# A self-planned hybrid decoder layer: state space kept in place, H by rows of both groups, and a planner with new costs

## The chip, the cores and the metric

The kernel runs on one core of a Trainium2 chip. Its metric is device time in microseconds, from the first to the last instruction as the host's timing of the device sees it; the time before is the median of 3 runs. TensorE (PE) multiplies matrices into PSUM, VectorE (DVE), ScalarE (ACT) and GpSimd (POOL) do the element-wise work, SyncE (SP) issues nearly all DMAs, in one queue and in order.

## The reference

One decoder layer on x of 2048 rows by 1024 (float32), one batch. After an RMSNorm one projection gives q, k, v (512 columns each) and u (512):

```python
proj = hn @ w_in[l]
q, k, v, u = jnp.split(proj, [QK_WIDTH, 2 * QK_WIDTH, 2 * QK_WIDTH + V_WIDTH], axis=-1)
q = partial_rope(...); k = partial_rope(...)          # first 16 of 64 columns rotated
attn = diff_attention(q, k, v, lam)                   # 4 heads, two softmax maps each, p0 - lam * p1, causal
attn = rms_norm(attn, subln_g[l]) * (1.0 - lambda_init)
ssm = s5_mixer(u, ...)
mixed = jnp.concatenate([attn, ssm], axis=-1) @ w_out[l]
h = h + mixed
hn = rms_norm(h, norm2_g[l])
h = h + (jax.nn.silu(hn @ w_gate[l]) * (hn @ w_up[l])) @ w_down[l]
return rms_norm(h, final_g)
```

The state space mixer has 32 groups of 16 channels; each drives a 64-wide complex diagonal state by a scan over positions. Then y = Re(C state) + D u, GELU, and a gate: `y * sigmoid(y @ w_glu + b_glu)`.

## The kernel before

All products in float32 are split into a high and a low part (`split`: ACT copies the high part, DVE subtracts) and made of three matmuls (`mm3`, lines 488 to 490).

**The planner.** The Python program does not write instructions in their final order. `Sched` holds tasks with an engine (or a choice of engines), a cost in microseconds, a priority and rings of buffers that they take and give; `run` simulates the engines with these costs, with `LAT0` and `MORE0` as latencies between engines and a formula for DMAs, and issues each task's instructions as its simulated turn comes. Each engine then executes its own list strictly in that order and waits on semaphores. `Rec` records the code of the first phase (projection and state space) as such tasks, with costs by a formula in `call`; all its instructions carry line 349 in the profile, so there one goes by tiles: `pair`, `pv`, `fx`, `tp` are PSUM banks, `hn` and `misc` SBUF areas that are carved again in each stage.

**Projection and state space** (`phase1`). Priorities run: norm, u's columns, tables of the state space (`ssm_prep`, two halves of 16 groups), 16 pairs of groups (`ssm_pair`), then the columns of q and k without rotation, those of v in two halves of 256, and last the rotated columns of q and k. As TensorE needs little time for the state space, the projection's matmuls stand between its pieces. A pair n loads u, G, H, T and E; TensorE makes z = G u (into `pv`) and y = T u (into `fx`); ACT copies z's halves so that real and imaginary parts stand together; DVE multiplies with cosine and sine tables that POOL builds, scans, multiplies back and writes the state into a PSUM bank (`tp`) in four instructions on 64 partitions that also swap the halves of odd and even groups; the state is split, TensorE adds H times the state to y, GELU goes to `yD` in DRAM. T is loaded into a scratch tile and copied by POOL in another order. Positions are blocked: index s (0 to 7) inside a step, c (0 to 255) over steps, position 8c + s.

**Gate** (`glu`). In 8 blocks b of 256 positions: four loads of y (line 1433) gather, for 128 channels each, 8 pieces of 32 numbers per channel; matmuls with w_glu; Tanh and a product (line 1474) write through a permuted view into the order of positions; `mixD`. The output projection's second half (`outproj(1, ...)`, with x added, result in `hD`) follows; these have low priority and fill gaps of attention.

**Attention** (`scores`, `values`). By head and block of 256 queries, for 128 queries at a time: scores into a PSUM pair, row maxima on DVE (line 1167), Exp on ACT (line 1182). Over 1024 keys a row has two pieces; ACT makes the factor between their maxima (line 1185), DVE adds the sums (lines 1201, 1203), forms the factor of the second map (1208, 1209) and, for the first piece, another (1212). Mixes of 512 columns (lines 1227 to 1235) join both maps on DVE or POOL, whichever the planner expects to be ready sooner. Transposes (line 1264), a split and products with v follow. q is loaded by four DMAs into one of two tiles (line 1102), k by line 1107, v by line 1112.

**After attention.** `outproj(0, ...)` reads `hD`, adds attention's half, and `norm2` norms and transposes; the FFN works by Strassen's scheme on halves (lines 1613 on) and the planner orders it in the same way.

Of the kernel before, what the change touches and what calls it, by code (L numbers as in the profile page):

```python
# [20 lines left out]
S = 2048  # L21
# [13 lines left out]
MORE0 = dict(pe=dict(dve=0.07, act=0.13, pool=0.12), pool=dict(dve=0.07))  # L35
# [136 lines left out]
class Sched:  # L172
# [13 lines left out]
    def __call__(self, engs, cost, fn, *deps, take=(), give=(), pri=0.0, size=0, stream=0, of=(), bias=BIAS):  # L186
# [62 lines left out]
    def run(self, until=None):  # L249
        while until is None or not until.done:  # L250
# [31 lines left out]
class Rec:  # L282


    def __init__(self, S, nc):
        self.S, self.real, self.pri, self.mem, self.open = S, nc, 0.0, {}, []
        self.areas, self.turned = {}, {}
# [78 lines left out]
    def call(self, eng, f, args, kw):  # L366
# [27 lines left out]
        if f == "tensor_tensor_scan":  # L394
            cost["dve"] *= 1.0
        if kw.get("op") == ALU.pow:
            cost["pool"] += 0.25 + 0.09 * n
        if eng == "any":
            return self.task({e: cost[e] for e in ("dve", "pool")}, [c])
# [70 lines left out]
class K:  # L470
# [72 lines left out]
    def setup(self, ctx):  # L543
# [10 lines left out]
        self.mixD = d("mixD", [128, 16, 8, 128])  # L554
        self.GHD = [d(f"GHD{i}", [128, 16, 2, 2, 128]) for i in range(2)]
# [39 lines left out]
    def phase1(self):  # L595
# [115 lines left out]
        rec.pri = -50.0  # L711
# [6 lines left out]
        rec.pri = -40.0  # L718
# [38 lines left out]
        for b in range(NB):  # L757
# [3 lines left out]
            for key in (("q", 0), ("k", 0)):  # L761
                t = proj(key, b, mm[2:4])
# [10 lines left out]
            self.hn_end.append(S.join(*rec.users(*(a.tile for a in self.hnb[b]))))  # L773
# [61 lines left out]
    def ssm_prep(self, pp, hf):  # L835
# [9 lines left out]
        if True:  # L845
# [87 lines left out]
            for q0 in range(0, NG, 2):  # L933
# [23 lines left out]
                nc.sync.dma_start(out=self.GHD[hf][:, gs], in_=gh.bitcast(F32))  # L957
# [4 lines left out]
            wh = view(self.gh2[0][:, 0:512], [128, 2] + B3[1:], F32R)  # L962
            self.split(wh[:, 0], wh[:, 1], wt)
            nc.sync.dma_start(out=self.WD[hf][112:240], in_=wh.bitcast(F32).rearrange("p j g h -> p j (g h)"))
# [5 lines left out]
    def ssm_pair(self, n):  # L970
# [11 lines left out]
        for i, z in enumerate((G, H)):  # L982
            nc.sync.dma_start(out=z.bitcast(F32), in_=self.GHD[hf][:, 2 * n8:2 * n8 + 2, i])
        if n % 2 == 0:

            self.T = s1.tile([128, 2, 4, 8, 16], F32R, name="sT")
            wd = self.WD[hf]
            for j in range(2):
                tr = s2.tile([128, 8, 4, 16], F32, name="tr")
                src = bass.AP(tensor=wd.tensor, offset=256 * j + 32 * n8, ap=[[512, 128], [16 * 512, 8], [1, 64]])  # L990
# [39 lines left out]
        v.tensor_tensor(out=t2, in0=pq, in1=Sb, op=ALU.mult)  # L1030
# [3 lines left out]
        for i in range(2):  # L1034
            v.tensor_tensor_scan(out=pq[:, i], data0=r, data1=t1[:, i], initial=0.0, op0=ALU.mult, op1=ALU.add)
        t1 = s2.tile(P3, F32, name="t1")
        t2 = s2.tile(P3, F32, name="t2")
        v.tensor_tensor(out=t1, in0=pq, in1=Cb, op=ALU.mult)
        v.tensor_tensor(out=t2, in0=pq, in1=Sb, op=ALU.mult)
# [7 lines left out]
        self.split(xh[:, :, 1:], xl[:, :, 1:], xs[:, :, 0:255])  # L1047
# [3 lines left out]
        a_.activation(out=gy, in_=y, func=AF.Gelu_apprx_tanh)  # L1051
# [4 lines left out]
    def phase2(self, upto=9):  # L1056
# [60 lines left out]
        def scores(pri, q, kk, j, t, l1c, over):  # L1117
# [12 lines left out]
            for ms in ((0, 1),) if L <= 512 else ((0,), (1,)):  # L1130
                for ci, c0 in enumerate(range(0, lt, 1024)):
# [27 lines left out]
                    def top(y, x=x, ms=ms, ci=ci, w=w):  # L1159
# [8 lines left out]
                        if ci:  # L1168
                            v.tensor_tensor(out=nl[:, i:i + 1], in0=nl[:, i - 1:i], in1=nl[:, i:i + 1], op=ALU.min)

                    y = S("dve", len(ms) * w * 1.042e-3 + 0.06 + (0.2 if ci else 0.0), top, x,
                          take=[] if first else [stats], pri=pri)
                    if not first:
                        first.append(y)
                    rings = [(U if ci else P)[m] for m in ms]

                    def exp(z, x=x, ms=ms, ci=ci, w=w, rings=rings):
# [6 lines left out]
                        if ci:  # L1184
# [894 lines left out]
```

## Time and profile before

| what | value |
|---|---|
| median of 3 runs | 2558.77 us (2556.92 to 2560.48) |
| the profiled execution | 2562.99 us, span 2561.2 us, granted clock 0.97 |
| q1, nearly all DMAs | 304464 packets, 384.39 MB, 48.0% of 16 engines |
| HBM | 259.08 MB read, 129.70 MB written |

The profile is of one execution. Busy time is the union of an engine's instructions; a group's row gives count, busy us and mean ns, then idle time just before the group and what ended it. Rows of the timeline give start and duration in us, engine, line, operation, output<-inputs, and in brackets the wait before. Rows of one line's instructions give minimum/median/maximum ns and the first and last start. A wait is put down to the semaphore that came last. The granted clock is the share of TensorE's full clock that it was given.

### The profile page before, as it was taken

The numbers are of one execution on the slowest core, as the hardware profiler recorded it, in microseconds if no ns is written. First come the engines' busy times: TensorE is split into PE (matmuls) and PEld (weight loads), VectorE is DVE, ScalarE is ACT, GpSimd is POOL, SyncE is SP. The second block draws the span as 40 slices with busy tenths as digits, with TensorE's granted clock in tenths as the row PEclk, the third lists the DMA queues.
The fourth block names the chain that finished last, engine by engine and source line by source line (L and its number), as shares of the span: only waits on it lengthen the run. The fifth ranks groups of instructions, "written<-read, shape, count | busy, mean of one in ns | idle before, by whom it ended". The sixth has DMA issues, their size and how long they took to land.

```text
span 2561.2 us, 34139 instructions
## 1 busy us (share of the span) xinstructions
PE 2355.5 (92%) x11736; PEld 1955.0 (76%) x11736; DVE 1805.1 (70%) x2898; ACT 997.5 (39%) x1971; POOL 1015.3 (40%) x1013
## 2 busy tenths in 40 slices
PE   7998789878998998997999999899999989989997
PEld 6787678757887777876788888788888867868775
DVE  7886884157999987558655655775655686695886
ACT  6222332246666555345333333343333332332343
POOL 4323561345665555336422222432222234253252
PEclk9999899989999999999999999999999989999999
DMA  5556675555547558588422222332222235555553
GB/s 196 163 173 213 193 211 156 152 179 156 138 140 222 169 174 233 180 290 275 127 83 73 93 82 82 116 116 83 83 87 79 85 125 172 178 181 165 187 173 126
DMA packets 307230, 391.03 MB, mean 153 GB/s; under 512 B 71984, under 2 KB 209264, under 8 KB 307056
## 3 DMA queue, kind: packets, MB, share of 16 engines
q1 hardware_dynamic: 304464, 384.39, 48.0%
q10 hardware_dynamic: 2592, 4.45, 0.5%
q8 instruction: 93, 1.52, 0.2%
q14 instruction: 81, 0.66, 0.1%
HBM read 259.08 MB, written 129.70 MB: 152 GB/s over the span
## 4 chain that ended last, share of the span: by engine, by line
PE 59%; DVE 19%; DMA 10%; issue 4%; POOL 3%; ACT 2%; SPq 1%; POOLq 0%; ACTq 0%; DVEq 0%
PE pair L488 8%; PE pair L489 8%; PE pair L490 8%; PE pair L349 6%; PE tp L490 3%; PE tp L489 3%; PE tp L488 3%; DVE misc L349 3%; DMA misc<-uD 3%; PE fx L488 2%; PE pv L490 2%; PE pv L489 2%; PE pv L488 2%; PE fx L490 2%; PE fx L489 2%
## 5 line engine op out<-in xcount | busy, mean ns | idle before, releaser
L1708 ACT CAST misc<-hn 128x512 fp32r<-128x512 f32 (+1 forms) x340 | 202.9, 609 | 479.4 <-POOL hn L1772 198.7
L488 PE MATMUL pair<-hn,misc 128*128 128x512 f32 x925 | 365.0, 395 | 17.2 <-DVE misc L1997 8.6
L490 PE MATMUL pair<-hn,misc 128*128 128x512 f32 x925 | 364.7, 394 | 8.3 <-DVE misc L1709 8.3
L489 PE MATMUL pair<-hn,misc 128*128 128x512 f32 x925 | 364.7, 394 | 7.6 <-DVE hn L1709 7.6
L1709 DVE TENSOR_TENSOR misc<-hn,misc 128x512 fp32r<-128x512 f32 (+1 forms) x340 | 250.6, 744 | 136.0 <-ACT misc L1708 135.7
L349 PE MATMUL pair<-hn,misc 128*128 128x512 f32 x1152 | 283.9, 402 | 2.6 <-DVE misc L349 2.6
L349 PEld LDWEIGHTS pair<-hn,misc 128*128 128x128 f32 x1152 | 219.0, 193 | 51.1 <-DVE misc L349 3.7
L488 PEld LDWEIGHTS pair<-hn,misc 128*128 128x128 f32 x925 | 176.0, 190 | 57.7 <-ACT misc L2006 8.5
L1182 ACT ACTIVATE hn<-pair,small 128x1024 f32<-128x1024 f32 (+4 forms) x192 | 166.3, 868 | 134.8 <-DVE small L1167 72.4
L489 PEld LDWEIGHTS pair<-hn,misc 128*128 128x128 f32 x925 | 176.0, 190 | 47.6 <-DVE hn L1709 11.3
L490 PEld LDWEIGHTS pair<-hn,misc 128*128 128x128 f32 x925 | 175.9, 190 | 47.7 <-DVE misc L1709 11.4
L1772 POOL TENSOR_TENSOR hn<-misc,hn 128x512 f32<-128x512 f32 (+1 forms) x68 | 90.8, 1335 | 283.4 <-DVE misc L1709 277.3
L1769 POOL TENSOR_TENSOR misc<-hn 128x512 f32<-128x512 f32 (+1 forms) x68 | 87.8, 1291 | 256.5 <-DVE misc L1709 191.9
L489 PE MATMUL tp<-hn,misc 128*128 128x512 f32 x457 | 179.8, 393 | 5.8 <-DVE hn L1709 5.8
L1779 POOL TENSOR_TENSOR hn<-hn 128x512 f32<-128x512 f32 (+1 forms) x68 | 95.7, 1407 | 221.3 <-DVE misc L1709 221.3
L488 PE MATMUL tp<-hn,misc 128*128 128x512 f32 x457 | 179.7, 393 | 1.2 <-ACT misc L2006 1.2
L490 PE MATMUL tp<-hn,misc 128*128 128x512 f32 x457 | 179.4, 393 | 0.9 <-DVE misc L1709 0.9
L1820 DVE TENSOR_TENSOR misc<-pair,misc 128x512 f32<-128x512 f32 x156 | 106.9, 688 | 99.7 <-PE pair L490 99.7
L1167 DVE TENSOR_REDUCE small<-pair 128x1 f32<-128x1024 f32 (+7 forms) x160 | 157.6, 988 | 21.8 <-PE pair L1149 11.5
L1229 POOL TENSOR_SCALAR hn<-hn,small 128x512 f32<-128x512 f32 (+3 forms) x105 | 80.8, 769 | 193.7 <-DVE small L1209 137.9
L349 POOL TENSOR_TENSOR misc<-misc 128x256 f32<-128x256 f32 (+1 forms) x128 | 116.8, 921 | 51.3 <-DVE misc L349 27.6
L349 DVE TENSOR_TENSOR misc<-misc,misc 128x512 f32<-128x512 f32 (+5 forms) x122 | 88.9, 754 | 52.0 <-ACT misc L349 47.4
(268 smaller groups left out, 5777.4 us busy)
## 6 DMA issues: line engine op xcount, KB each, us to landing
hn<-vD SPq DMA_DIRECT2D x48, 512.0 KB
hn<-kD SPq DMA_DIRECT2D x96, 256.0 KB
hn<-in_w_gate SPq DMA_DIRECT2D x44, 512.0 KB
hn<-in_w_up SPq DMA_DIRECT2D x44, 512.0 KB
fD<-misc SPq DMA_DIRECT2D x88, 256.0 KB
hn<-qD SPq DMA_DIRECT2D x128, 128.0 KB
hD<-misc SPq DMA_DIRECT2D x32, 512.0 KB
misc<-hD SPq DMA_DIRECT2D x32, 512.0 KB
```

Of the source, the lines that this page charges most:

```text
L349: getattr(ENGINE[t.at](self.real), f)(*map(now, args), **{n: now(x) for n, x in kw.items()})
L488: nc.tensor.matmul(out, lhsT=ah, rhs=bh, start=start, stop=False, **k)
L489: nc.tensor.matmul(out, lhsT=ah, rhs=bl, start=False, stop=False, **k)
L490: nc.tensor.matmul(out, lhsT=al, rhs=bh, start=False, stop=stop, **k)
L1167: v.tensor_reduce(out=nl[:, i:i + 1], in_=x.got[sc][:, 0:w], axis=AX.X, op=ALU.max, negate=True)
L1182: a_.activation(out=z.got[rings[i]][:, 0:w], in_=x.got[sc][:, 512 * i:512 * i + w], func=AF.Exp, bias=st(n, n + 1), accum_out=acc)
L1708: hf = lambda t: a_.copy(out=dst(t)[0], in_=src())
L1709: lf = lambda t: (g_ if t.at == "pool" else v).tensor_sub(out=dst(t)[1], in0=src(), in1=dst(t)[0].bitcast(F32))
L1769: s1 = any_(n, lambda t, e: e.tensor_tensor(out=t.got[s1r][:, 0:n], in0=q(1, 0), in1=q(1, 1), op=ALU.add), *r, take=[s1r], pri=pri())
L1772: s2 = any_(n, lambda t, e: e.tensor_sub(out=q(0, 0), in0=s1.got[s1r][:, 0:n], in1=q(0, 0)), s1, s3, a11, pri=pri())
L1779: s4 = any_(n, lambda t, e: e.tensor_sub(out=q(0, 1), in0=q(0, 1), in1=q(0, 0)), s2, a12, pri=pri())
L1820: return S("dve", 1.042e-3 * w + 0.07, lambda t: v.tensor_tensor(out=(t if to is None else to).got[tm], in0=x.got[bank], in1=y.got[tm], op ...
```

## The change

1. **Planner.** Latencies to TensorE are raised by 0.1 us, each task of the other engines costs 0.09 to 0.13 more, DMAs are counted slower, and the costs of recorded instructions get a formula by kind and by use of PSUM. Choices between DVE and POOL in the state space use the factor `FAIR` (1.2 on DVE) in place of `BIAS` (4).
2. **State space.** The scan and the multiplication back stay in SBUF tiles of all 128 partitions: no state in PSUM and no swap. H is stored as rows of both groups (`HD`), and H's product runs on 64 rows at a time, two halves per group. y of the two groups stands in two banks (`fx`, and the `tp` bank that the state had). T is stored so that its load needs no copy; its weights are read with a step of four. The multiplications by sine may run on DVE or POOL. `ssm_prep` stores G once and H twice where it stored both at once.
3. **Projection's end.** The second half of v's columns goes behind the rotated columns of q and k.
4. **Gate.** A block b is now the index s of the position, so that y comes in one load of pieces of 256 numbers, nothing is permuted, and the result goes to `sD`. The output projection's tile i takes rows z, s (every eighth position); its first part waits for the eight stores of its half.
5. **Attention.** ACT adds the sums, POOL forms the factor of the second map, the separate factor (1212) is gone, and the scaling of the first map's first piece becomes a task of its own on ACT or POOL.

```diff
-MORE0 = dict(pe=dict(dve=0.07, act=0.13, pool=0.12), pool=dict(dve=0.07))
+MORE0 = dict(pe=dict(dve=0.17, act=0.23, pool=0.22), pool=dict(dve=0.07))
+STEP = dict(dve=0.09, act=0.09, pool=0.13)
...
-                self.dma = max(self.dma, s + 1.1) + t.size / 3.6e5
-                t.end = self.dma + 0.95
+                self.dma = max(self.dma, s + 1.5) + t.size / 2.8e5
+                t.end = self.dma + 1.5
...
-        cost = dict(dve=1.042e-3 * n + 0.07, act=0.88e-3 * n + (0.16 if "accum_out" in kw else 0.08),
-                    pool=(1.1e-3 if f == "tensor_scalar" else 0.3e-3 if f == "memset" else 2.2e-3) * n + 0.1)
+        if f == "tensor_tensor_scan" or psum[0]:
+            dve = 2.3e-3 * n + 0.03
+        elif f in ("tensor_scalar", "memset"):
+            dve = 0.75e-3 * n + 0.03
+        else:
+            dve = 1.06e-3 * n + 0.06 if any(psum) else 1.27e-3 * n + 0.02
+        cost = dict(dve=dve, act=0.87e-3 * n + (0.26 if "accum_out" in kw else 0.08),
+                    pool=(1.0e-3 if f == "tensor_scalar" else 0.3e-3 if f == "memset" else 2.0e-3) * n + 0.12)
... # ssm_prep
-                nc.sync.dma_start(out=self.GHD[hf][:, gs], in_=gh.bitcast(F32))
+                nc.sync.dma_start(out=self.GD[hf][:, gs], in_=gh[:, :, 0])
+                for f in range(2):
+                    nc.sync.dma_start(out=self.HD[hf][gs, :, f].rearrange("g p x -> p g x"),
+                                      in_=gh[64 * f:64 * f + 64, :, 1])
... # ssm_pair
-                tr = s2.tile([128, 8, 4, 16], F32, name="tr")
-                nc.sync.dma_start(out=tr.rearrange("p s g h -> p s (g h)"), in_=src)
-                g_.tensor_scalar(out=self.T[:, j].rearrange("p g s h -> p s g h"), in0=tr, scalar1=1.0, scalar2=1.0,
-                                 op0=ALU.mult, op1=ALU.mult)
+                nc.sync.dma_start(out=self.T[:, j].bitcast(F32).rearrange("p (s x) -> p s x", s=8), in_=src)
...
-        y = view(self.fx1, P3, F32)
+        y = [z[:, 0:256] for z in (self.fx1, self.tp2[1])]
-            self.mm3(y[:, g], T[:, 0, tg], T[:, 1, tg], u[:, g, :, 0], u[:, g, :, 1], g == 0, True, skip_group_check=True)
+            self.mm3(y[g], T[:, 0, tg::4], T[:, 1, tg::4], u[:, g, :, 0], u[:, g, :, 1], True, True)
...
-        v.tensor_tensor(out=t2, in0=pq, in1=Sb, op=ALU.mult)
-        xs = view(self.tp2[1], P3, F32)
-        v.tensor_tensor(out=xs[lo, 0], in0=t1[lo, 0], in1=t2[lo, 1], op=ALU.subtract)
-        v.tensor_tensor(out=xs[hi, 1], in0=t1[hi, 0], in1=t2[hi, 1], op=ALU.subtract)
-        v.tensor_tensor(out=xs[hi, 0], in0=t1[lo, 1], in1=t2[lo, 0], op=ALU.add)
-        v.tensor_tensor(out=xs[lo, 1], in0=t1[hi, 1], in1=t2[hi, 0], op=ALU.add)
+        nc.any.tensor_tensor(out=t2, in0=pq, in1=Sb, op=ALU.mult)
+        v.tensor_tensor(out=t1[:, 0], in0=t1[:, 0], in1=t2[:, 1], op=ALU.subtract)
+        v.tensor_tensor(out=t1[:, 1], in0=t1[:, 1], in1=t2[:, 0], op=ALU.add)
...
-            self.mm3(y[:, g], H[:, g, 0], H[:, g, 1], xh[:, g], xl[:, g], False, True, skip_group_check=True)
+            r = slice(64 * g, 64 * g + 64)
+            for f in range(2):
+                x = f ^ g
+                self.mm3(y[g], H[r, f, 0], H[r, f, 1], xh[r, x], xl[r, x], False, f == 1, skip_group_check=True)
+            nc.flush()
... # glu
-                for k in range(4):
-                    nc.sync.dma_start(out=y[:, k], in_=yv[128 * k:128 * k + 128, :, 32 * b:32 * b + 32])
-            x = S("sp", 1.88, load, *self.yst, take=[yr], pri=pri(), size=524288)
+            x = S("sp", 0.47, lambda t, b=b: nc.sync.dma_start(
+                out=t.got[yr], in_=yv[b].rearrange("(k p) c -> p k c", p=128)), *self.yst, take=[yr], pri=pri(),
+                size=524288)
... # scores
-                e0 = S("dve", 0.07, lambda _: v.scalar_tensor_tensor(
-                    out=l1c, in0=st(4, 5), scalar=st(8, 9), in1=st(5, 6), op0=ALU.mult, op1=ALU.add), exps[0, 1], pri=pri)
+                            a_.activation(out=st(7, 8) if m else l1c, in_=st(3 + n, 4 + n), func=AF.Identity,
+                                          scale=st(8 + m, 9 + m), bias=st(4 + n, 5 + n))
...
-            r = S("dve", 0.1, lambda _: v.scalar_tensor_tensor(
-                out=st(10, 11), in0=st(10, 11), scalar=nlam, in1=l1c, op0=ALU.mult, op1=ALU.mult), r, es[0], pri=pri)
+            r = S("pool", 0.14, lambda _: g_.tensor_scalar(
+                out=st(10, 11), in0=st(10, 11), scalar1=nlam, scalar2=l1c, op0=ALU.mult, op1=ALU.mult), r, es[0], pri=pri)
...
+                    def scaled(y, at=at):
+                        if y.at == "act":
+                            a_.activation(out=at(0), in_=at(0), func=AF.Copy, scale=st(8, 9))
+                        else:
+                            g_.tensor_scalar(out=at(0), in0=at(0), scalar1=st(8, 9), scalar2=1.0, op0=ALU.mult,
+                                             op1=ALU.mult)
+                    x0 = S(dict(act=0.6, pool=0.8), 0.0, scaled, es[0], pri=pri)
```

More of the change, by code (lines that the diff above doesn't have):

```diff
@@ L191, in __call__ @@
             t.engs = {engs: cost * 1.02}
+        else:
+            t.engs = {e: c + STEP.get(e, 0.0) for e, c in t.engs.items()}
         t.fn, t.pri, t.take, t.give, t.size, t.bias = fn, pri, take, give, size, bias
@@ L398, in call @@
         if eng == "any":
-            return self.task({e: cost[e] for e in ("dve", "pool")}, [c])
+            return self.task({e: cost[e] for e in ("dve", "pool")}, [c], bias=FAIR if self.fair else BIAS)
         return self.task((eng, cost[eng]), [c])
@@ L553, in setup @@
         self.yD = d("yD", [8, 16, 16, 2, 256])
-        self.mixD = d("mixD", [128, 16, 8, 128])
-        self.GHD = [d(f"GHD{i}", [128, 16, 2, 2, 128]) for i in range(2)]
+        self.mixD = d("mixD", [128, 16, 4, 128])
+        self.sD = d("sD", [128, 8, 4, 256])
+        self.GD = [d(f"GD{i}", [128, 16, 256]) for i in range(2)]
+        self.HD = [d(f"HD{i}", [16, 64, 2, 256]) for i in range(2)]
         self.WD = [d(f"WD{i}", [240, 2, 256]) for i in range(2)]
@@ L726, in phase1, with values @@
         self.vst = [[], []]
-        for hf in range(2):
+        def values(hf, banks):
             wload(("v", 2 * hf))
@@ L772, in phase1 @@
                 store(key, b, z)
-            self.hn_end.append(S.join(*rec.users(*(a.tile for a in self.hnb[b]))))
+        values(1, mm[2:4])
+        self.hn_end = [S.join(*rec.users(*(a.tile for a in self.hnb[b]))) for b in range(NB)]
         self.nc = nc
@@ L961, in ssm_prep @@
             v.tensor_tensor(out=wt, in0=wt, in1=wps, op=ALU.add)
-            wh = view(self.gh2[0][:, 0:512], [128, 2] + B3[1:], F32R)
-            self.split(wh[:, 0], wh[:, 1], wt)
-            nc.sync.dma_start(out=self.WD[hf][112:240], in_=wh.bitcast(F32).rearrange("p j g h -> p j (g h)"))
+            wh = view(self.gh2[0][:, 0:512], [128, 2, 4, 64], F32R)
+            for i in range(4):
+                h, l = (wh[:, j, i].rearrange("p (h g) -> p g h", g=4) for j in range(2))
+                self.split(h, l, wt[:, 4 * i:4 * i + 4])
+            nc.sync.dma_start(out=self.WD[hf][112:240], in_=wh.bitcast(F32).rearrange("p j q x -> p j (q x)"))
             w2 = pp.tile([128, 256], F32, name="w2", tag="w2")
@@ L1223, in mix @@
+                def mix(y, at=at, part=part):
                     e = g_ if y.at == "pool" else v
-                    x0, x1 = (p(m, c0 // 1024)[:, c0 % 1024:c0 % 1024 + wd] for m in range(2))
-                    c2 = st(11, 12) if part else st(10, 11)
                     if e is v and not part:
-                        v.scalar_tensor_tensor(out=x0, in0=x1, scalar=c2, in1=x0, op0=ALU.mult, op1=ALU.add)
+                        v.scalar_tensor_tensor(out=at(0), in0=at(1), scalar=st(10, 11), in1=at(0), op0=ALU.mult, op1=ALU.add)
@@ L1237, in scores @@
-                cost = dict(pool=(4.91e-3 if part else 3.6e-3) * wd + 0.1, dve=(2.0e-3 if part else 1.1e-3) * wd + 0.1)
-                pieces.append(S(cost, 0.0, mix, r2 if part else r, pri=pri))
+                    e.tensor_scalar(out=at(1), in0=at(1), scalar1=st(10, 11), scalar2=st(9, 10) if part else 1.0,
+                                    op0=ALU.mult, op1=ALU.mult)
+                    e.tensor_tensor(out=at(0), in0=at(0), in1=at(1), op=ALU.add)
+                cost = dict(pool=4.1e-3 * wd + 0.1, dve=(2.5e-3 if part else 1.6e-3) * wd + 0.1)
@@ L1239, in scores @@
+                pieces.append(S(cost, 0.0, mix, r, x0, pri=pri))
                 if t == 0 and c0 + 512 >= lt:
@@ L1557, in operands @@
             hl = S("sp", 0.47, lambda t: nc.sync.dma_start(
-                out=t.got[ohr], in_=(A["x"] if part else self.hD)[128 * i:128 * i + 128, :]),
-                None if part else self.stored[i], take=[ohr], pri=pri(), size=524288)
+                out=t.got[ohr], in_=rows(A["x"] if part else self.hD, i)),
+                None if part else self.held[i // 8], take=[ohr], pri=pri(), size=524288)
             return mx, hl
@@ L1584, in half @@
                 give=[(fx, own)], pri=pri())
-        step = 2
+        step, held = 2, []
         for i0 in range(lo, hi, step):
@@ L1599, in outproj @@
                     hl = ops[i][1]
-                    self.stored[i] = S("sp", 0.47, lambda _, i=i, hl=hl: nc.sync.dma_start(
-                        out=self.hD[128 * i:128 * i + 128, :], in_=hl.got[ohr]), *sums[i], pri=pri(), size=524288,
-                        give=[(ohr, hl)])
+                    held.append(S("sp", 0.47, lambda _, i=i, hl=hl: nc.sync.dma_start(
+                        out=rows(self.hD, i), in_=hl.got[ohr]), *sums[i], pri=pri(), size=524288,
+                        give=[(ohr, hl)]))
+        if part:
+            self.held = [S.join(*held[8 * z:8 * z + 8]) for z in range(2)]
     def norm2(self, i, pri, hl, sums):
```

98 lines of the change are left out of this document (45 added, 53 removed).

## The prediction

> **What bounds the kernel now.** The page comes first: its engine line and the forty slices of TensorE.
>
> ```profile
> span 2561.2 us, 34139 instructions
> PE 2355.5 (92%) x11736; PEld 1955.0 (76%) x11736; DVE 1805.1 (70%) x2898; ACT 997.5 (39%) x1971; POOL 1015.3 (40%) x1013
> PE   7998789878998998997999999899999989989997
> ```
>
> TensorE is busy 2355.5 of 2561.2 us, so all that an order can win is the 205.7 us in which it stands, plus what a lower clock adds to its busy time. The windows by stage say where that is: the columns are stretch, length, busy time of PE, PEld, DVE, ACT and POOL with instruction counts, granted clock, DMA share, GB/s.
>
> ```profile
> 0.00:225.00 225.00, 202.11 (x975) 164.37 (x976) 180.91 (x465) 82.30 (x150) 72.79 (x108) 1.00 0.56 188
> 225.00:410.00 185.00, 147.23 (x869) 129.75 (x869) 151.26 (x244) 55.96 (x124) 96.60 (x112) 0.92 0.65 192
> 410.00:520.00 110.00, 102.32 (x611) 88.44 (x610) 19.89 (x34) 22.60 (x42) 22.99 (x18) 0.97 0.53 165
> 520.00:660.00 140.00, 108.46 (x695) 92.14 (x693) 99.49 (x184) 75.09 (x191) 71.62 (x81) 0.88 0.54 150
> 660.00:1090.00 430.00, 398.05 (x2521) 340.87 (x2520) 358.67 (x644) 245.40 (x549) 235.19 (x269) 0.98 0.60 183
> 1090.00:1230.00 140.00, 120.97 (x560) 96.41 (x558) 92.43 (x95) 68.61 (x124) 71.51 (x67) 0.94 0.83 275
> 1230.00:2561.00 1331.00, 1276.39 (x5516) 1043.05 (x5515) 902.44 (x1237) 447.50 (x794) 444.58 (x359) 0.98 0.37 118
> ```
>
> The rows are: norm and tables; state space with projection as filler; the projection's end; attention's start with the gate; attention; output projection; FFN. TensorE stands 37.8 us in the second, 7.7 in the third, 31.5 in the fourth, 32.0 in the fifth, 19.0 in the sixth, 54.6 in the last. The change edits the second to fifth, 109 us. Who makes TensorE wait there is in the table of waits (total us, times, longest), here for 225:410, 410:520, 520:660 and 660:1090 in that order:
>
> ```profile
> PE pv L349 <- DMA misc<-uD: 27.6, 22, 4.4
> ...
> PE tp L349 <- ACT misc L349: 5.7, 4, 4.1
> ...
> PE pair L1145 <- DMA hn<-qD: 19.3, 7, 5.4
> ...
> PE pair L1145 <- DMA hn<-qD: 7.8, 3, 5.7
> PE tp L1264 <- POOL hn L1235: 6.7, 4, 4.6
> PE tp L1264 <- DVE hn L1273: 6.4, 12, 1.3
> ```
>
> Two late loads, u of the state space and q of attention, make 54.7 us of the 109. DVE is the second bound of attention: 358.67 of 430.
>
> **The state space (225 to 410).** Its matmuls are an obligation inside a stream of projection matmuls that would run anyway; the stage's price is TensorE's work plus its stalls, not the length of the chain of a pair. The timeline shows a pair's u loads and the matmuls that wait for them, then two matmuls of the gate, back to back:
>
> ```profile
> 298.93 1.28 SPq L349 DMA_DIRECT2D misc<-uD  x2
> 304.11 0.62 PE L349 MATMUL pv<-misc 128*128 128x256 f32 x3 [0.93 <-DMA misc<-uD]
> 307.34 1.95 SPq L349 DMA_DIRECT2D misc<-uD  x2
> 314.90 1.01 PE L349 MATMUL pv<-misc 128*128 128x256 f32 x3 [2.91 <-DMA misc<-uD]
> 521.25 0.28 PE L489 MATMUL fx<-misc,misc 128*128 128x256 f32 x1
> 521.36 0.28 PE L490 MATMUL fx<-misc,misc 128*128 128x256 f32 x1
> ```
>
> From issue to use is 5.2 us in one and 7.6 us in the other. The planner counts a 256 KB load at 1.1 + 262144/3.6e5 + 0.95 = 2.78 us, the changed one at 1.5 + 262144/2.8e5 + 1.5 = 3.94. It therefore puts z's matmuls some 1.16 us later behind filler, which is at hand (the stage behind is projection too). 22 waits of 1.25 us mean could lose up to 1.16 each, 25.5 us; loads stay later than planned and some waits are longer, so I take half, -13 (ends 0 and -27.6).
>
> H's product is the cost. With the state kept in place each group's H holds 64 rows for each of two halves, so a pair has 12 H matmuls in place of 6: 16 x 6 = 96 more. Spacing by the two rows is 0.11 to 0.12 us: +11.5. No row shows a matmul of 64 rows. From below: the two halves of the array overlap fully, 0. From above: each of the 32 groups also pays the tail of a matmul, 0.28 - 0.12 = 0.16 us, on entering and on leaving, +10.2, so +22. I take +11.5, the spacing being the nearest row. T's weights are now read four elements apart (96 loads). No row shows that: 0 if they stay hidden, +11.5 if each costs one more spacing; I take 0 since weight loads run ahead.
>
> The Trainium skill, TensorEngine Tiling (Array Packing), Key Properties, speaks against this edit: changing the tiling mode drains TensorE. No row here shows it; by it the sum would be the upper end, some 10 us more.
>
> DVE and POOL get lighter:
>
> ```profile
> L349 DVE TENSOR_TENSOR tp<-misc 64x256 f32<-64x256 f32 x64 | 38.5, 601 | 2.0
> L349 DVE TENSOR_TENSOR misc<-misc 128x256 f32<-128x256 f32 x33 | 17.4, 564 | 0.1
> L349 POOL TENSOR_SCALAR misc<-misc 128x512 fp32r<-128x512 f32 x16 | 10.7, 671 | 59.3 <-DMA misc<-GHD 29.4 <-DMA misc<-WD 21.9 <-PE fx L349 7.2
> ```
>
> 64 writes into PSUM (38.5 us) become 32 of 128x256 at 0.564 (18.0): -20 us of DVE. The 16 copies of T leave POOL (-10.7), and t2 may move from DVE to POOL. DVE fills 151.26 of 185 here and is not who TensorE waits for: I count nothing, -10 as the far end if the faster pace lets u load sooner. The second Gelu call, split G and H loads and 32 further stores in preparation lie on ACT and SP beside TensorE work (the stores' price stands with SP's queue below). Half the stalls gone also lifts the clock, 0.92 now: 3 of the 147 x 0.08 = 12 us. Stage: -13 + 11.5 - 3 = -4.5.
>
> **The projection's end.** Rotating q and k of the first columns leaves TensorE waiting (5.7, ACT). The second half of the values, 384 matmuls, moves behind it and fills that. The stores of q and k land earlier, those of v for heads 2 and 3 later, with two heads of attention as cover. Freeing hn, block by block, stays spread over some 45 us. -5 (ends 0 and -7.7).
>
> **Attention's start.** All loads go through SP's queue, in order. Its timeline, two lines of the code, SP's wait for a q buffer, and two of TensorE's waits:
>
> ```profile
> 542.07 7.84 SPq L1433 DMA_DIRECT2D misc<-yD  x4
> 564.06 7.42 SPq L1433 DMA_DIRECT2D misc<-yD  x4
> 583.46 9.57 SPq L1433 DMA_DIRECT2D misc<-yD  x4
> ...
> L1433 SPq DMA_DIRECT2D misc<-yD x32: 359/680/3693, 473.6 to 700.0; - x32
> ...
> L1112 SPq DMA_DIRECT2D hn<-vD x48: 359/371/3223, 471.9 to 1033.5; - x48
> ...
> SPq L1102 <- PE pair L1149: 24.8, 14, 3.5
> ...
> 559.16 0.66 PE L1145 MATMUL pair<-hn 128*128 128x384 f32 x1 [5.45 <-DMA hn<-qD]
> 580.21 0.66 PE L1145 MATMUL pair<-hn 128*128 128x384 f32 x1 [5.26 <-DMA hn<-qD]
> ```
>
> Three y loads hold SP for 24.8 us; behind each stands a q load, and the two longest waits, 5.45 and 5.26, follow them. The old load takes 4 issues of 1024 pieces of 128 bytes; the new one is one issue of 512 pieces of 1 KB, the shape of a v load, median 0.371. 24.8 becomes 1.1. (At the same 0.371 the 32 stores in preparation take 12 us of SP, under projection matmuls; uncovered they would cost those 12.) Of the 19.3 us of q waits I take -15 (ends -4, when only the buffer's release counts, and -19.3). Clock 0.88: 108 x 0.12 = 13 us lost, half comes back, -6. Stage: -21.
>
> **Attention.** What moves off DVE (ns minimum/median/maximum), and the add of POOL's mixes:
>
> ```profile
> L1201 DVE SCALAR_TENSOR_TENSOR small<-small x32: 201/580/1299, 598.8 to 949.9; 128x1 f32<-128x1 f32 x32
> L1203 DVE SCALAR_TENSOR_TENSOR small<-small x32: 205/218/1030, 603.3 to 953.7; 128x1 f32<-128x1 f32 x32
> L1209 DVE SCALAR_TENSOR_TENSOR small<-small x64: 202/219/1239, 522.8 to 1052.3; 128x1 f32<-128x1 f32 x64
> L1212 DVE TENSOR_TENSOR small<-small x32: 141/159/1142, 605.9 to 955.2; 128x1 f32<-128x1 f32 x32
> L1474 DVE SCALAR_TENSOR_TENSOR misc<-misc,misc x22: 605/631/1735, 535.3 to 787.1; 128x256 f32<-128x256 f32 x22
> L1185 ACT ACTIVATE small<-small x64: 281/284/326, 598.5 to 952.2; 128x1 f32<-128x1 f32 x64
> ...
> L1235 POOL TENSOR_TENSOR hn<-hn 128x512 f32<-128x512 f32 (+2 forms) x44 | 56.4, 1282 | 3.7
> ```
>
> By medians: 32 x 0.58 + 32 x 0.218 + 64 x 0.219 + 32 x 0.159 = 44.6 us, and the gate's 32 strided halves at 0.631 (20.2) become 16 whole rows, about 0.65 as an estimate, -10: 55 us of DVE over 570. ACT takes 64 small activations, 64 x 0.284 = 18 us, and a share of 64 scalings at the planner's 0.6, 38 us at most, beside 245 busy of 430; POOL takes 64 products and loses the other scalings. DVE's waits (6.4), POOL's (6.7) and q's (7.8) are what can shrink; of 20.9 I take -8 (ends -20 and +20, the product below). The eight stores that the second pass now waits for precede it by its place in the rings: 0.
>
> **The rest.** Output projection and FFN keep their work; the planner's raised costs (0.1 us more from any engine to TensorE, 0.09 to 0.13 on each step of the others) only reorder. TensorE is full there for long stretches: 0, with 10 either way.
>
> **Sum:** -4.5 - 5 - 21 - 8 = -38.5 against the profiled execution's 2562.99, 2524.5; that execution lies 4.2 above the median 2558.77, so the median goes to 2520.
>
> **Rivals.** *q is held by its buffer.* SP waits 24.8 us for scores to release a q tile, so freeing SP gives the start only -5: sum -22.5, 2536. Against: the two longest waits sit right behind y loads.
>
> *The state space pays more.* Drains and T's weights cost +22 + 11.5 and the uD stalls go down by 13 all the same: +20.5 in place of -4.5, 2545; with no stall recovered, 2558. For: no row shows these forms. Against: PE there is half filler.
>
> *Slower: the factor's product on POOL.* It leaves DVE for POOL, in order behind mixes whose add alone is 1.28 us, and every mix of its tile waits for it, then the transposes. 64 tiles: at 0.6 us each unhidden the gains are gone; at 1.0 us, +64 - 38.5, the time is 2584. For: TensorE already waits 6.7 on POOL. Against: POOL is at 55% and other matmuls fill in.
>
> *Slower: the new order opens stalls in the FFN*, doubling its 54.6: 2575.
>
> **How the numbers follow.** Forecast 0.50; q buffer 0.17; state space 0.15, half of it within 0.2%; POOL 0.13; FFN 0.05. Two tenths of a per cent, 5 us, is about what a measurement of this kernel tells from no change. Faster 0.50 + 0.17 + 0.07, same 0.08, slower 0.18. The forecast's own range is 2495 to 2540; leaving out a tenth on each side, with the state space's far end in and the POOL case out, gives 2488 to 2562.
>
> **What would show it.** Eight y issues of under half a microsecond; q waits in the 140 us after the projection's end under 8; u waits near 14; 192 H matmuls on 64 rows, at 0.12 spacing or with gaps at their edges; DVE in attention some 45 lower; idle time before POOL's mixes not grown. It fails if u's waits stay at 27, if H's product leaves gaps, or if TensorE's waits for POOL or ACT in attention rise past 30.

## The result and the profile after

The changed kernel takes **2523.59 us** (median; 2521.86 to 2525.93) where the kernel before, on the same chip, takes 2559.31: a ratio of **0.9866**, 95% interval 0.9853 to 0.9878, so 36 us. The forecast was 2520. The total came out as said, by luck as the last sections show: the terms that make it did not, and the experiments are about that.

The page of the changed kernel, its engine line:

```profile
span 2522.1 us, 34209 instructions
PE 2355.8 (93%) x11832; PEld 1965.3 (78%) x11832; DVE 1721.8 (68%) x2637; ACT 1048.8 (42%) x2098; POOL 1081.8 (43%) x1078
```

TensorE is as busy as before (2355.8 against 2355.5) and stands 166.3 us in place of 205.7. To see where, both spans are cut at the same marks of each kernel: the last H product, the projection's last matmul, the last product with v, the first matmul of the FFN, the end. Windows of before, then of after, with the columns of the prediction's windows:

```profile
0.00:412.00 412.00, 351.34 (x1859) 296.10 (x1860) 332.85 (x707) 138.26 (x273) 169.40 (x220) 0.96 0.60 190
412.00:530.00 118.00, 108.49 (x637) 92.27 (x635) 24.33 (x44) 26.54 (x55) 27.21 (x24) 0.96 0.54 170
530.00:1059.00 529.00, 467.35 (x3026) 401.24 (x3026) 444.33 (x803) 312.06 (x718) 296.25 (x339) 0.95 0.58 171
1059.00:1219.00 160.00, 143.14 (x678) 116.84 (x678) 94.92 (x103) 68.78 (x125) 71.37 (x70) 0.96 0.81 271
1219.00:2561.00 1342.00, 1285.22 (x5544) 1048.59 (x5542) 908.65 (x1243) 451.84 (x802) 451.06 (x363) 0.98 0.37 118
```

```profile
0.00:441.00 441.00, 392.84 (x2050) 333.74 (x2050) 324.72 (x666) 145.93 (x300) 187.15 (x224) 0.94 0.61 182
441.00:558.00 117.00, 99.47 (x640) 87.31 (x640) 29.47 (x50) 33.24 (x79) 40.83 (x43) 0.91 0.54 171
558.00:1085.00 527.00, 496.86 (x3167) 428.48 (x3167) 390.44 (x619) 362.19 (x818) 314.94 (x379) 0.97 0.62 196
1085.00:1202.00 117.00, 89.27 (x437) 71.75 (x436) 74.50 (x76) 54.89 (x101) 52.86 (x55) 0.88 0.73 242
1202.00:2522.00 1320.00, 1277.38 (x5544) 1044.01 (x5543) 902.72 (x1228) 452.53 (x802) 486.06 (x378) 0.99 0.37 120
```

Length less PE's busy time is what TensorE stands. In order, before: 60.7, 9.5, 61.7, 16.9, 56.8. After: 48.2, 17.5, 30.1, 27.7, 42.6. Two rows contradict the forecast at once. The FFN, of which no line is edited and which was entered at 0, is 22 us shorter with the same 5544 matmuls. The projection's end, which was to win 5, stands 8 us longer. So only 17 of the 39 us of the span lie ahead of the FFN, where the sum had put all of it.

The table of waits of after, whole span:

```profile
PE fx L497 <- ACT misc L1739: 15.9, 2, 12.4
PE tp L353 <- ACT misc L353: 15.6, 6, 6.5
...
PE pair L1171 <- DMA hn<-qD: 7.6, 4, 2.7
PE fx L353 <- DMA misc<-uD: 7.3, 1, 7.3
...
PE tp L1292 <- POOL hn L1263: 2.9, 5, 0.8
...
PE pv L353 <- DMA misc<-uD: 2.1, 4, 0.7
```

Waits for u fell from 27.6 to 9.4 (7.3 and 2.1), those for q from 27.1 (19.3 and 7.8) to 7.6. Of the two rows on top the first, at the FFN's start, is new; the second, at the projection's end, was 5.7 before. The y loads of after, in SP's rows:

```profile
L1459 SPq DMA_DIRECT2D misc<-yD x8: 359/380/2066, 483.1 to 633.2; - x8
```

Eight issues with a median of 0.38 us, the longest 2.07, where before 32 issues stood.

### The profile page after: what moved, and what is told of

Its sections match the earlier page's. It is cut to its first block, busy times and chain, and to the rows that moved or that the text cites. A ratio compares the mean times of both kernels' runs of the same rounds, so it can differ in the third digit from the quotient of the medians.

```text
span 2522.1 us, 34209 instructions
## 1 busy us (share of the span) xinstructions
PE 2355.8 (93%) x11832; PEld 1965.3 (78%) x11832; DVE 1721.8 (68%) x2637; ACT 1048.8 (42%) x2098; POOL 1081.8 (43%) x1078
## 5 line engine op out<-in xcount | busy, mean ns | idle before, releaser
L498 PE MATMUL pair<-hn,misc 128*128 128x512 f32 x924 | 362.9, 393 | 7.1 <-DVE hn L1740 6.9
L497 PE MATMUL pair<-hn,misc 128*128 128x512 f32 x924 | 361.8, 392 | 5.4 <-ACT misc L1739 2.1
L499 PE MATMUL pair<-hn,misc 128*128 128x512 f32 x924 | 362.1, 392 | 4.6 <-DVE misc L1740 4.6
L353 PE MATMUL pair<-hn,misc 128*128 128x512 f32 x1152 | 277.3, 396 | 1.3 <-DVE misc L353 1.3
L353 PEld LDWEIGHTS pair<-hn,misc 128*128 128x128 f32 x1152 | 214.0, 189 | 46.0 <-DVE misc L353 1.8
L498 PEld LDWEIGHTS pair<-hn,misc 128*128 128x128 f32 x924 | 174.1, 188 | 48.5 <-DVE hn L1740 13.0
L497 PEld LDWEIGHTS pair<-hn,misc 128*128 128x128 f32 x924 | 174.2, 189 | 43.8 <-issue 2.7
L499 PEld LDWEIGHTS pair<-hn,misc 128*128 128x128 f32 x924 | 174.2, 189 | 43.4 <-DVE misc L1740 7.9
L1209 ACT ACTIVATE hn<-pair,small 128x1024 f32<-128x1024 f32 (+4 forms) x192 | 166.3, 868 | 72.1 <-DVE small L1200 35.9
L353 POOL TENSOR_TENSOR misc<-misc,misc 128x256 f32<-128x256 f32 (+1 forms) x64 | 65.3, 1020 | 183.2 <-DVE misc L353 164.5
L353 DVE TENSOR_TENSOR misc<-misc,misc 128x512 f32<-128x512 f32 (+7 forms) x124 | 108.3, 899 | 38.3 <-ACT misc L353 36.5
```

Of the source, the lines that this page charges most:

```text
L353: getattr(ENGINE[t.at](self.real), f)(*map(now, args), **{n: now(x) for n, x in kw.items()})
L497: nc.tensor.matmul(out, lhsT=ah, rhs=bh, start=start, stop=False, **k)
L498: nc.tensor.matmul(out, lhsT=ah, rhs=bl, start=False, stop=False, **k)
L499: nc.tensor.matmul(out, lhsT=al, rhs=bh, start=False, stop=stop, **k)
L1209: a_.activation(out=z.got[rings[i]][:, 0:w], in_=x.got[sc][:, 512 * i:512 * i + w], func=AF.Exp, bias=st(n, n + 1), accum_out=acc)
```

## The experiments

The change falls into five parts that can be made alone: planner's numbers (P), state space (S), values' order (V), gate (G), attention (A).

**One part at a time.** P alone is the kernel before with the new numbers; the others keep the old planner.

```diff
  # P alone: before, and
+MORE0 = dict(pe=dict(dve=0.17, act=0.23, pool=0.22), pool=dict(dve=0.07))
+STEP = dict(dve=0.09, act=0.09, pool=0.13)
+                self.dma = max(self.dma, s + 1.5) + t.size / 2.8e5
...
  # all but P: after, and
-STEP = dict(dve=0.09, act=0.09, pool=0.13)
...
  # G alone: before, and (glu, the rows of outproj)
+            x = S("sp", 0.47, lambda t, b=b: nc.sync.dma_start(
+                out=t.got[yr], in_=yv[b].rearrange("(k p) c -> p k c", p=128)), *self.yst, take=[yr], pri=pri(),
+                size=524288)
...
  # A alone: before, and (scores)
+            r = S("pool", 0.14, lambda _: g_.tensor_scalar(
+                out=st(10, 11), in0=st(10, 11), scalar1=nlam, scalar2=l1c, op0=ALU.mult, op1=ALU.mult), r, es[0], pri=pri)
...
  # S alone: before, and (ssm_prep, ssm_pair, FAIR)
+                self.mm3(y[g], H[r, f, 0], H[r, f, 1], xh[r, x], xl[r, x], False, f == 1, skip_group_check=True)
...
```

P alone and all but P have every number of the planner, the DMA formula and the costs of recorded instructions among them, new and old respectively.

> The kernel before with the planner's new numbers alone: latencies to TensorE, the step on each task, the DMA formula and the costs of recorded instructions. Theory A, that of the prediction: an order of the same work, nothing in output projection and FFN, at most u's waits in the state space fall from 27.6 to about 14 us: 2545 to 2560 us. Theory B, from the two traces: the FFN's 5544 matmuls took 1333.2 us from first to last start before and 1311.2 after, though no line of the FFN changed, so the new numbers give some 22 us there, and with u's waits 2525 to 2540 us.

> The changed kernel with the planner's old numbers; the other four parts stay. Theory A: 2520 to 2535 us, the gain stays, since it lies in the gate's load and in attention. Theory B: the FFN goes back to its old 1333 us from first to last matmul and the time is 2540 to 2555 us.

> The kernel before with the gate's part alone: one load of y per block, sD, rows by z and s. Theory A: q's waits fall from 27.1 to under 12 us and the clock of attention's start rises: 2535 to 2545 us. Theory B: the wait is passed on to q's buffer or to the exponentials, 2548 to 2560 us. In both SP spends about 5 us on y's loads where it spent 42.7.

> The kernel before with attention's part alone: sums on ACT, the factor on POOL, scaling on ACT or POOL. Theory A: DVE's busy time falls by some 45 us and the time to 2545 to 2555 us. Theory B, the slower rival of the prediction: the factor waits in POOL's queue behind mixes, TensorE's waits for POOL in attention rise past 20 us, 2565 us or more.

> The kernel before with the state space's part alone: state in place, H on 64 rows, T read with a step of four, sine products on DVE or POOL. Theory A: the H products' 11.5 us against u's waits, without the planner's later loads: 2555 to 2570 us. Theory B, from the changed kernel's trace (three T matmuls start to start 0.68 us where they took 0.36, 96 of them: 10 us more; DVE gains nothing beside POOL): 2570 to 2590 us.

| kernel | median us | ratio to before (95%) |
|---|---|---|
| P alone | 2552.97 | 0.9968 (0.9955 to 0.9981) |
| all but P | 2563.27 | 1.0013 (1.0000 to 1.0026) |
| G alone | 2546.31 | 0.9950 (0.9932 to 0.9967) |
| A alone | 2544.39 | 0.9944 (0.9925 to 0.9963) |
| S alone | 2580.10 | 1.0083 (1.0067 to 1.0099) |

Without the planner's numbers the whole change is worth nothing (2.6 us slower than before): on top of the other parts they bring 40 us, alone 8. Where P works shows in the windows of P alone from its first FFN matmul on, and of the kernel with all but P:

```profile
1230.00:2550.00 1320.00, 1278.11 (x5544) 1044.05 (x5544) 899.45 (x1228) 452.71 (x803) 486.85 (x378) 0.99 0.38 120
```

```profile
1213.00:2557.00 1344.00, 1289.04 (x5544) 1050.12 (x5544) 908.47 (x1243) 452.26 (x804) 452.68 (x363) 0.98 0.37 118
```

The FFN takes 1320 us with the new numbers, in P alone as in after, and 1342 to 1349 with the old, in before, all but P and S alone (its windows follow). P alone pays half of that back: its first FFN matmul is at 1230, 11 us later than before. So its time lies in theory A's range though B had the FFN right; all but P has B's FFN and is 8 us above its range. u's waits fall to 10.8 us in P alone, as the forecast expected of the planner's numbers.

Attention alone does what it says. Window 520:1090 of before, of A alone, of after:

```profile
520.00:1090.00 570.00, 506.51 (x3213) 433.01 (x3212) 458.16 (x828) 320.50 (x739) 306.81 (x350) 0.95 0.59 175
```

```profile
520.00:1090.00 570.00, 519.62 (x3279) 444.67 (x3278) 411.14 (x660) 378.50 (x861) 324.24 (x396) 0.96 0.60 184
```

```profile
520.00:1090.00 570.00, 538.09 (x3474) 467.25 (x3474) 403.95 (x646) 380.97 (x869) 329.59 (x402) 0.97 0.62 197
```

DVE is 47 us lower in A alone, ACT 58 higher, and TensorE does 13 us more in the same stretch. Its time is just under theory A's range; that of G alone lies between its two theories. The waits for q stay in A alone (26.5) and fall to 17.2 in G alone. G and A together do not bring them to the 7.6 of after: the two kernels below that have both and the values in the old order keep 17.9 (e6) and 16.3 (e9). The last 10 us or so hang on the values' order.

S alone is the loss, as theory B had it. Its windows up to the last H product and to the projection's last matmul, and the sum over its span:

```profile
0.00:410.00 410.00, 353.08 (x1804) 294.50 (x1804) 307.50 (x660) 140.28 (x289) 175.98 (x219) 0.96 0.63 187
410.00:542.00 132.00, 123.44 (x785) 108.93 (x784) 26.80 (x50) 28.01 (x60) 27.06 (x24) 0.99 0.51 162
...
sum 2578.00, PE 2379.24 PEld 1973.04 DVE 1784.23 ACT 1002.23 POOL 1022.51; mean PE 475.85 PEld 394.61 DVE 356.85 ACT 200.45 POOL 204.50
```

DVE is 25 us lower up to the last H product, as the edit says, and the state space ends only 2 us earlier. TensorE's work grows by 23.7 us over the span (2379.2 against 2355.5), 16.7 of them in these two rows (353.08 + 123.44 against 351.34 + 108.49); the projection's last matmul comes 12 us later. 6 more lie in the FFN, which no edit of S touches. Two kinds of matmul make most of it. T's six products in before, with the projection's next matmul; then rows of after: T's products into `fx` and `tp`, projection, G's into `pv`, and further on a burst of H's on 64 rows between projection matmuls:

```profile
306.79 0.88 PE L349 MATMUL fx<-misc,misc 128*128 128x256 f32 x6
307.50 2.46 PE L349 MATMUL pair<-hn,misc 128*128 128x512 f32 x10
```

```profile
314.25 0.86 PE L353 MATMUL fx<-misc,misc 128*128 128x256 f32 x3
314.94 0.86 PE L353 MATMUL tp<-misc,misc 128*128 128x256 f32 x3
315.64 1.72 PE L353 MATMUL pair<-misc,hn 128*128 128x256 f32 x13
317.20 0.52 PE L353 MATMUL pv<-misc 128*128 128x256 f32 x3
317.56 1.72 PE L353 MATMUL pair<-misc,hn 128*128 128x256 f32 x13
...
322.48 0.40 PE L353 MATMUL pair<-misc,hn 128*128 128x256 f32 x2
322.81 0.66 PE L353 MATMUL fx<-misc,misc 64*128 64x256 f32 x3
...
323.42 0.28 PE L353 MATMUL tp<-misc,misc 64*128 64x256 f32 x1
323.43 0.28 PE L353 MATMUL fx<-misc,misc 64*128 64x256 f32 x1
...
323.66 0.51 PE L353 MATMUL tp<-misc,misc 64*128 64x256 f32 x3
324.10 1.57 PE L353 MATMUL pair<-misc,hn 128*128 128x256 f32 x11
```

From a group of T's three to what follows pass 0.69 and 0.70 us, 0.23 each. Before, six took 0.71, 0.12 each, and G's three in after, whose weights have no step, take 0.36, again 0.12. 96 of T's at 0.11 more are some 11 us. (Where the granted clock is low the step hides: at 0.57, from 346 to 349 us, G's three and T's three alike take 0.63 to 0.68.)

H's burst has gaps at its edges. The last projection matmul before it starts at 322.48 + 0.40 - 0.28 = 322.60 and the first on 64 rows at 322.81, the last of these at 323.66 + 0.51 - 0.28 = 323.89 and the next projection matmul at 324.10: both times 0.21 us where 0.12 is the usual step. The whole burst of twelve takes 324.10 - 322.60 = 1.50 us between two projection matmuls; six, in seven steps of 0.12, would make that 0.84. 16 bursts like this one would be some 11 us more, 3 of them gaps. Together 21 by this estimate, where 16.7 were measured in the two stages; a step that falls into a wait or a stretch of low clock costs less.

**The values put back, and more of the same.** e6 is after with the second half of the values ahead of the rotated columns again, as before. e8 is after with the four blocks of q ahead of those of k.

```diff
  # e6: after, and
-        def values(hf, banks):
+        for hf in range(2):
...
-        values(1, mm[2:4])
  # e8: after, and
-        for b in range(NB):
-            for key in (("q", 0), ("k", 0)):
+        for key in (("q", 0), ("k", 0)):
+            for b in range(NB):
```

> The changed kernel with the values' second half back in front of the rotated columns. Theory A: the change of order brought 5 us, so this takes 2526 to 2532 us. Theory B: in the changed kernel TensorE waits 6.5 and 5.2 us at 475 and 483 us, when the weights of the values wait for a buffer that the first q unit holds until its last matmul; the reorder brought nothing or cost some: 2510 to 2523 us.

> The changed kernel with all four blocks of the first q unit ahead of those of the first k unit (the two tables are loaded twice, eight loads more), so that the values' last weights find a free buffer 22 us earlier. Theory B: the waits of 6.5 and 5.2 us go, 2510 to 2516 us. Theory A: the rotation's chain itself is what TensorE waits for, 2521 to 2527 us.

e6: **2507.77, ratio 0.9800 (0.9782 to 0.9817)**, under both ranges. V costs 16 us, where the forecast had it win 5. Windows 400:441 of after and of e6, all instructions, then e6's projection matmuls alone (those into `pair`; after has none there):

```profile
400.00:441.00 41.00, 25.89 (x104) 20.66 (x104) 28.88 (x41) 11.69 (x29) 21.72 (x20) 0.58 0.53 138
```

```profile
400.00:441.00 41.00, 39.42 (x303) 37.88 (x302) 29.97 (x48) 14.24 (x38) 19.62 (x20) 1.00 0.71 196
...
400.00:441.00 41.00, 27.00 (x213) 25.96 (x212) 3.70 (x9) 3.60 (x10) 1.00 0.71 196
```

The last pairs of the state space need something for TensorE to do between their pieces. In e6 27 of 41 us are projection matmuls, the values. In after these are held back, the filler has run out, TensorE stands 15 us and its granted clock is 0.58. At the projection's end, where the values were to fill, TensorE stands more than without them, 17.5 us against 7.0 in e6 (its window 443:520):

```profile
475.40 2.07 PE L353 MATMUL tp<-misc,cst 128*128 128x512 f32 x2 [6.47 <-ACT misc L353]
482.68 2.07 PE L353 MATMUL tp<-misc,cst 128*128 128x512 f32 x2 [5.21 <-ACT misc L353]
```

These two waits of after, for a rotation's input, are most of the new 15.6; the values follow behind them in TensorE's order and cannot pass. Up to the projection's last matmul V so costs 20 us of standing; attention gives 10 back (30.1 us in after's third window, 40.3 in e6's 520:1056), where q's waits are the 7.6 and 17.9 of above. Why the order moves q's waits was not traced.

e8: 2518.09, 0.9843 (0.9828 to 0.9858), between its two ranges and 5.5 us under after. Its wait of `tp` for ACT is again 15.6, so the gain isn't there; its FFN starts 7 us earlier, and what of the order did that isn't settled.

**T copied by POOL again, and the sine on DVE.**

```diff
  # e7: after, and
+                nc.sync.dma_start(out=tr.rearrange("p s g h -> p s (g h)"), in_=src)
+                g_.tensor_scalar(out=self.T[:, j].rearrange("p g s h -> p s g h"), in0=tr, scalar1=1.0, scalar2=1.0,
+                                 op0=ALU.mult, op1=ALU.mult)
  # e10: e6, and, twice
-        nc.any.tensor_tensor(out=t2, in0=pq, in1=Sb, op=ALU.mult)
+        v.tensor_tensor(out=t2, in0=pq, in1=Sb, op=ALU.mult)
```

> The changed kernel with T loaded into scratch and copied by POOL as before, so that its weights are read in one run instead of with a step of four. Theory A (the step is hidden): no gain, 2523 to 2530 us, since POOL has 16 copies of 0.67 us more. Theory B (each of 96 T matmuls pays some 0.11 us for its weights): weight loads of T back to 0.2 from 0.32 us, 2510 to 2518 us.

> The changed kernel with the values in the old order and both sine products of a pair always on DVE. Theory A (DVE is short in the state space and POOL's help is worth it): 2510 to 2520 us. Theory B (DVE's products with two SBUF inputs slow down while POOL works, 1.12 us for 512 columns against 0.64 alone, so POOL's help is paid back): 2503 to 2510 us, with the mean of DVE's 512-column products under 1.0 us.

e7: 2566.18, 1.0026 (1.0015 to 1.0037), 43 us above after and far above both ranges. It cannot price the strided weights by its time: the copies come on top of the sine products that POOL now has, and `fx` waits 18.9 us for POOL. Its weight loads of T do tell. Before, after and e7, weight loads of 225:440:

```profile
L349 PEld LDWEIGHTS fx<-misc,misc 128*128 128x128 f32 x192 | 28.0, 204 | 4.8 <-ACT misc L349 2.1 <-DVE misc L349 1.1 <-POOL misc L349 0.9
```

```profile
L353 PEld LDWEIGHTS fx<-misc,misc 128*128 128x128 f32 x52 | 13.2, 315 | 10.7 <-DMA misc<-uD 7.7 <-ACT misc L353 2.5 <-issue 0.2
```

```profile
L353 PEld LDWEIGHTS fx<-misc,misc 128*128 128x128 f32 x42 | 7.6, 232 | 11.2 <-POOL misc L353 10.9 <-DVE misc L353 0.2
```

With a step of four elements the mean load of a 128x128 float32 tile takes 0.315 us, without it 0.20 to 0.23; with the step gone e7's loads are back, as theory B said of them.

e10: 2524.40, 0.9861 (0.9840 to 0.9882), 17 us above e6 and above both ranges: to let POOL take a share of the sine products is worth that, though each product on DVE is faster without POOL beside it. DVE's rows of 225:440, the same 128x512 product in before, after and e10:

```profile
L349 DVE TENSOR_TENSOR misc<-misc,misc 128x512 f32<-128x512 f32 x64 | 49.7, 815 | 18.0 <-ACT misc L349 14.0 <-POOL misc L349 3.1
```

```profile
L353 DVE TENSOR_TENSOR misc<-misc,misc 128x512 f32<-128x512 f32 x44 | 48.5, 1121 | 9.8 <-ACT misc L353 8.3 <-POOL misc L353 1.1
```

```profile
L353 DVE TENSOR_TENSOR misc<-misc,misc 128x512 f32<-128x512 f32 x64 | 48.7, 800 | 28.0 <-ACT misc L353 20.8 <-POOL misc L353 7.0
```

44 products cost after as much as 64 cost the others: 20 products moved to POOL took nothing off DVE (49.7 and 48.5 us). DVE's relief shrinks with it: up to the last H product S alone had 25 us less on DVE than before, after has 8 (324.72 against 332.85). Why the time falls all the same when POOL takes a share was not traced further. The Trainium skill, SBUF — State Buffer, Who interferes with whom, says that a DVE instruction with two SBUF inputs contends with a GpSimd instruction that reads SBUF. The rows agree: 0.80 to 0.82 us becomes 1.12 where POOL has more of this work. So do the single products of before in this stretch: the 25 that an instruction of POOL overlaps for over 80% of their time take 1.03 us in the median, the 22 that it overlaps for less than 5% take 0.68.

**The state space taken out.** e9 is P, G and A, with state space and values as before.

```diff
  # e9: before, and the lines of P alone, G alone and A alone
+STEP = dict(dve=0.09, act=0.09, pool=0.13)
...
```

> Planner, gate and attention as changed; state space and the order of the values as before. It stands against the changed kernel with the values in the old order, 2507.8 us, in which the state space is new. Theory A: the new state space costs TensorE 96 products of H and slower weight loads of T, as it did alone (2580 against 2559), and without it the time is 2490 to 2500 us. Theory B: with the planner's new numbers the old state space runs long (ends at 461 us with the planner alone, 443 with all but the values) and is what phase one waits for, 2510 to 2520 us.

2508.54, 0.9799 (0.9779 to 0.9820), between its two ranges: the same as e6, which has S as well. The sums of e9's and e6's windows:

```profile
sum 2504.00, PE 2338.84 PEld 1954.89 DVE 1717.71 ACT 1044.69 POOL 1064.09; mean PE 334.12 PEld 279.27 DVE 245.39 ACT 149.24 POOL 152.01
```

```profile
sum 2508.00, PE 2357.55 PEld 1967.85 DVE 1725.74 ACT 1049.40 POOL 1073.45; mean PE 471.51 PEld 393.57 DVE 345.15 ACT 209.88 POOL 214.69
```

S adds 18.7 us to TensorE's work, of the size of T's and H's 21 above, and takes 165.2 - 150.5 = 14.7 off its standing. It nets nothing.

**Which number of the planner.** From e6, one of them goes back: `MORE0` in e11, `STEP` in e12.

```diff
  # e11: e6, and
-MORE0 = dict(pe=dict(dve=0.17, act=0.23, pool=0.22), pool=dict(dve=0.07))
+MORE0 = dict(pe=dict(dve=0.07, act=0.13, pool=0.12), pool=dict(dve=0.07))
  # e12: e6, and
-STEP = dict(dve=0.09, act=0.09, pool=0.13)
+STEP = {}
```

> The changed kernel with the values in the old order and the latencies to TensorE at their old values. Theory A: the FFN's gain comes from the latencies, so the FFN goes back from 1322 to some 1340 us: 2520 to 2530 us. Theory B: it comes from the step on the other engines' tasks, the FFN stays at 1322 and the time at 2503 to 2512 us; the one wait of 9 to 12 us at the FFN's start may go with the latencies, then 2495 to 2503.

> The changed kernel with the values in the old order and no step added to the tasks of DVE, ACT and POOL. Theory A: the FFN's gain comes from the latencies and the time stays at 2505 to 2512 us. Theory B: it comes from the step: FFN back to 1335 to 1343 us, 2520 to 2535 us.

e11: **2506.02, 0.9785 (0.9762 to 0.9808)**, the fastest kernel of the study and no different from e6 by the intervals. e12: 2544.79, 0.9939 (0.9920 to 0.9958), 37 us above e6 and above both ranges. So 0.09 to 0.13 us per task decide nearly all of the 40 us that the planner's numbers bring (those were measured with the values moved), and the raised latency nothing. The FFN of e12, and who makes TensorE wait in it:

```profile
1203.00:2543.00 1340.00, 1289.38 (x5544) 1050.77 (x5544) 906.45 (x1242) 453.60 (x803) 456.67 (x364) 0.98 0.36 118
```

```profile
PE pair L497 <- ACT misc L1735: 17.6, 4, 14.6
...
PE pair L497 <- DVE misc L2024: 11.9, 5, 3.4
```

Its 1340 are back near the old 1342, 18 us over e6's 1322, and the FFN starts 17 us later than in e6 (1203, 1186): the step acts in both halves of the kernel. In the FFN TensorE stands 50.6 us, in e6 40.5, and works 8 us longer at a clock of 0.98 in place of 0.99. The waits for the FFN's last adds (line 2024) are 11.9 us into `pair`; in after (its line 2028) they are 1.9 there and 4.2 into `pv`. That is some 6 of the 10; the rest was not traced. What stays in every kernel with new numbers, e12 too, is the wait for ACT at the FFN's start (longest 14.6 here, 12.4 in after); it is neither from `STEP` nor from `MORE0` (9.4 in e11). The DMA formula and the costs of recorded instructions were not separated.

## Why the prediction was right in the total and wrong in its terms

| term | forecast us | measured us |
|---|---|---|
| state space | -4.5 | +21 alone, -1 beside the new planner (e6 less e9) |
| projection's end | -5 | +16 (after less e6) |
| attention's start: gate | -21 | -14 alone |
| attention | -8 | -16 alone |
| the rest: planner's numbers | 0 ± 10 | -8 alone, -40 beside the others; FFN -22 |
| sum | -38.5 | -36 |

The measured column does not add up by itself: P, G and A make -38 one by one and -52 together.

- **"The planner's raised costs" that "only reorder": the step that failed most.** To reorder is what can move the time when engines run in strict order: FFN idle falls from 56.8 to 42.6 us and its clock goes from 0.98 to 0.99. "TensorE is full there for long stretches" was read from a busy share, while the prediction's own windows showed 54.6 us of standing.
- **Projection's end: the cover was named and not counted.** The forecast put z's matmuls "behind filler, which is at hand (the stage behind is projection too)", and in the next term moved 384 of those filler matmuls away. Window 400:441 shows them missing. The two terms should have drawn on one stock.
- **State space.** Right: u's waits (9.4 left; 14 forecast), DVE's 20 us and that they are worth nothing (S alone), the price of 192 H matmuls (some 11 us where 11.5 were taken). Mis-sized: T's strided weights, taken as 0 "since weight loads run ahead", cost some 11, near the stated far end of 11.5. "The state space pays more", 2545 to 2558, is what S does under the old planner.
- **Drains.** By the Trainium skill, TensorEngine Tiling (Array Packing), Key Properties, a change of tiling mode drains TensorE. The rows agree that a change costs time: 0.21 us from a 128-row matmul to one of 64 rows and back, 0.12 without a change. The forecast named such gaps as a sign that it fails; they are 0.09 us each and some 3 us in all, not the 10.2 of its upper end. Whether a drain makes them or a weight load that comes late, the rows don't tell.
- **Attention's start.** SP's cause was right: the y loads fell to eight, q's waits in the gate alone from 27.1 to 17.2. The 7.6 of the changed kernel are not the gate's alone: with the values in the old order 17.9 remain. "q is held by its buffer" holds for a part: G alone wins 14, between the 5 of that rival and the 21 taken.
- **Attention.** DVE's relief was sized rightly (54 lower over 520:1090 in after, 45 and 10 forecast), its worth too low, 8 where 16 came. The rival of POOL's product fell: `tp` waits 2.9 us for POOL, 6.7 before.
- **FFN stalls** as a rival had the wrong sign; its one true part is the new wait of 12.4 at the FFN's start.

That 2520 held is luck, errors of both signs: the projection's end is 21 us worse than its term, the FFN 22 better.

## What to carry to other kernels

Where engines execute in order, the planner's costs are a part of the kernel: a tenth of a microsecond too little per task cost 37 us here, a stage with no edit won 22, so such a change is tried by itself, and once more on top of the rest: here 8 and 40 us. Filler is a stock: a block of independent work that is moved to fill one gap is missing where it stood, and the windows of that place show whether it was needed there (here 27 of 41 us). A step in a weight operand and a second SBUF input beside a busy POOL belong into the sum; a count of instructions alone had them at nothing.

## What the runs showed of the hardware

- A weight load of 128x128 float32 with a step of four elements takes 0.315 us in the mean, without 0.20 to 0.23; T's matmuls of 256 columns then come 0.23 us apart, not 0.12. At a granted clock of 0.57 G's matmuls, without a step, came no closer than 0.21 either.
- From a 128-row matmul to one of 64 rows, and back, pass 0.21 us where 0.12 is the usual step.
- Matmuls on the two 64-row halves run side by side: starts 0.01 us apart at 0.28 us each.
- A DVE product of 128x512 float32 with two inputs in SBUF takes 0.68 us in the median beside an idle POOL and 1.03 us beside a busy one (before, 225:440).
- With TensorE busy 25.89 of 41 us the granted clock in that window was 0.58, with 39.42 it was 1.00. The Trainium skill, TensorE: Matmul & The Clock Gate, Part 1, tells of a clock that is gated down when TensorE idles; the two windows agree, and its window length was not measured here.
